# The low half of the weights begins 224 instead of 160 bytes behind the high half, modulo 256

## The chip, the cores and the metric

The kernel runs on one core of a Trainium2 chip. The metric is the device time of one execution in microseconds; it is given as the median of several executions.

## What is computed

One step of a one-layer decoder with 288 tokens (256 of a prompt, 8 sequences of 4 new ones) of width 2048. Four sub-layers stand on one residual stream, and a norm ends it:

```python
h = h + 0.5 * ((silu(hn @ wg) * (hn @ wu)) @ wd)            # FFN 1, hn = rms_norm(h), inner width 5632
h = h + concat(rms_norm(conv_y), rms_norm(attn_o)) @ w_out  # token mixing: short conv, and attention
h = h + 0.5 * ((silu(hn @ wg) * (hn @ wu)) @ wd)            # FFN 2, weights of its own
h = h + sigmoid(hn @ w_ple_gate) * (p @ w_ple_proj)         # per-layer input
y = rms_norm(h)
```

In the token mixing one projection `hn @ w_in` gives the inputs of a gated convolution of width 3 and q, k, v and the forget gates of 8 heads of 128. The prompt attends causally to itself; each sequence attends to 1024 cached rows, gathered by pages, and to its new rows. Everything is float32.

## The kernel before

Activations lie transposed: 128 features on the partitions, the 288 tokens along the row (NT = 288). All large products go through one helper, `pair` (line 311). It makes two output blocks of 128 features (b = 0, 1) from weight tiles of 4 x 128 input features by 256 output features.

**Three products for one.** So that the array's fast float32 form (fp32r) loses no accuracy, each operand is split in a high and a low part. For each input block k and output block b there are three products into the same bank of PSUM, each with 288 moving columns and a load of 128 x 128 weights:

```python
for x in (xh, xl) if rows_first else (xl, xh):
    pe.matmul(o, hi[:, j % 2, w], x, start=f, stop=False)                              # line 338
    f = False
state["product"] = pe.matmul(o, lo[:, j % 2, w], xh, start=False, stop=l)              # line 340
```

In words: low rows on high weights, high rows on high weights, high rows on low weights; then the next k. Each product has a weight load of its own, so whi is loaded twice. While a product streams its rows, the weights of the next one are loaded: whi (again) under the first product of a triple, wlo under the second, the next whi under the third. There are 5,536 such triples. `rows_first`, the other order of the first two, is used for the first pair of FFN 1 alone.

**What moves.** x (`new_x`, tile `x`, 16 blocks) is the normed input of an FFN, of w_in and of the per-layer gate; `hid` (`ffn`) holds eight inner blocks of an FFN; `zc`, `za` are the two halves of the input of w_out, in single tiles of 288; `ph`, `plo` the per-layer input. x and hid are laid out by `both` (line 212): for each block 288 high elements and behind them 288 low ones, after a pad of BEFORE_X or BEFORE_H elements.

**What is loaded.** A weight tile comes from memory in one transfer (`wraw`, 512 KB). `split_weight` (line 292) turns each half of it into `whi` (a copy on ScalarE, rounded) and `wlo` (the difference, on VectorE). Five `whi` and five `wlo` are in turn, 2,048 bytes in a partition each. Both pools are made in `build`, with a tile that nothing uses between them:

```python
wsp = pool("wsp", HALVES)
pool("low").tile([P, LOWS], F32, name="gap")
wlp = pool("wlp", HALVES)
```

**Where things lie.** Pools are placed one behind the other in a partition: constants and h, x, wraw, whi, the gap, wlo, and above them what each stage opens (f1, tq, zq, mix, cv, f2, pl). In the placed program every whi begins at a multiple of 256 bytes and every wlo at 160 modulo 256 (LOWS = 40 elements of 4 bytes). A block of whi or wlo within its tile begins 512 or 1,024 bytes on, so this holds for each load. The high rows of x begin at 240 modulo 256 (BEFORE_X = 60) and the low ones 1,152 bytes on, at 112; a block is 2,304 bytes, nine times 256, so this holds for every k. hid begins at 160 modulo 256 and its pad is 80 bytes (BEFORE_H = 20): 240 and 112 as well. Of the tiles of w_out, zc has its high rows at 160 and its low ones at 32; za has both at 160 in even blocks and both at 32 in odd ones.

The order of the work on TensorE is that of the steps in `run_steps`, with the small products of attention put between (`between`, line 1012), and two products with `meanr` for each norm (`inv_rms`, line 190).

Of the kernel before, what the change touches and what calls it, by code (L numbers as in the profile page):

```python
# [42 lines left out]

RAW = 8
HALVES = 5
LOWS = 40
BEFORE_X = 60
BEFORE_H = 20
MANUAL = False
BANKS = dict(mm=3, kt=3, va=2)  # L50
KPAIRS = (1, 8, 14, 21, 27, 34, 40, 47)
# [44 lines left out]
def build(nc, tc, ctx, A, O):  # L96
    def pool(name, bufs=1, to=ctx, **k):
        return to.enter_context(tc.tile_pool(name=name, bufs=bufs, reuse_waits="tile", **k))
# [6 lines left out]
# [3 lines that stand above are left out]
# [104 lines left out]
    def both(p, name, blocks, before, **k):  # L212
        n = blocks * 2 * NT
        t = p.tile([P, (before + n + 63) // 64 * 64], F32R, name=name, tag=name, **k)
        t = t[:, before:before + n].rearrange("p (k s n) -> p s k n", s=2, n=NT)
        return t[:, 0], t[:, 1]
# [153 lines left out]
    def do(fn):  # L370
        steps.append(([], fn))
# [18 lines left out]
    def ffn(wg, wu, wd, nextgain, work):  # L390
# [3 lines left out]
        for gi, grp in enumerate(groups):  # L394
            firstg = gi == 0 and nextgain == "norm_mix"

            def start():
                H["hi"], H["lo"] = both(work(), "hid", 8, BEFORE_H, bufs=2)
            do(start)
# [847 lines left out]
```

## Time and profile before

| | |
|---|---|
| median of 3 executions | 2280.74 us |
| the three | 2279.36, 2280.74, 2295.28 us |
| the profiled execution, its own time | 2295.44 us |
| its span, first to last instruction | 2293.7 us |
| granted TensorE clock, mean | 0.998 |
| products on TensorE | 17,387 |
| FFN 1 | about 4 to 854 us of the span |
| w_in, attention, first half of w_out | about 854 to 1290 us |
| second half of w_out | about 1290 to 1341 us |
| FFN 2 | about 1341 to 2173 us |
| per-layer input, final norm | about 2173 to 2294 us |

How to read it: a group's row gives line, engine, operation, the tile written and the tiles read, the shape and the count; then its busy time, the mean duration of one in ns, and the idle time of the engine ahead of it. For a product the tiles read are the moving rows and the weights: `mm<-x,whi` has rows of x on high weights. x and hid stand for high and low rows alike. mm, kt and va are banks of PSUM. PEld is the weight load, which runs beside PE. A row of windows gives for a stretch (us from the start of the span) its length, the busy time with the number of instructions that run in it, the granted clock, the share of the DMA engines and GB/s. The row of a single line or tile gives the shortest, the median and the longest duration in ns. Products overlap in the array, and their ends are modelled.

### The profile page before, as it was taken

What the parts mean: (1) busy time and instruction counts of PE and PEld (TensorE: products, weight loads), DVE (VectorE), ACT (ScalarE), POOL (GpSimd) and SP (SyncE); (2) the same over time, 40 slices, a digit from 0 to 9 for tenths busy, and PEclk for the clock granted to TensorE, in tenths of its full rate; (3) what the DMA queues carried; (4) which work ended last, traced back from release to release, by engine and by line L of the source; (5) the groups of instructions that cost most, each with busy time, mean ns of one, the idle gap of its engine ahead of it and who ended that gap; (6) DMA issues with size and microseconds to landing.
All of it is one profiled execution on the core that took longest, in us unless ns stands there. A gap on an engine that the chain in (4) does not pass through costs nothing.

```text
span 2293.7 us, 44307 instructions
## 1 busy us (share of the span) xinstructions
PE 2280.6 (99%) x17387; PEld 2225.6 (97%) x17387; DVE 1344.6 (59%) x2413; ACT 1051.3 (46%) x1860; POOL 323.5 (14%) x398
## 2 busy tenths in 40 slices
PE   9999999999999999999999999999999999999997
PEld 9999999999999999989888999999999999999997
DVE  7555555555555586455557775555555555555855
ACT  6444444444444463333334554444444444444654
POOL 1020000000000023345446210000000000000110
PEclk9999999999999999999999999999999999999999
DMA  8575555555555556988888554645555555555552
GB/s 273 164 246 162 170 166 166 166 166 166 165 166 166 166 164 206 346 298 297 317 317 299 183 169 150 187 155 183 172 169 167 173 166 170 171 166 172 169 170 88
DMA packets 342865, 443.37 MB, mean 193 GB/s; under 512 B 17424, under 2 KB 307104, under 8 KB 342656
## 3 DMA queue, kind: packets, MB, share of 16 engines
q1 hardware_dynamic: 320944, 366.25, 49.7%
q0 software_dynamic: 20480, 71.67, 9.0%
q8 instruction: 136, 2.23, 0.4%
q10 hardware_dynamic: 1232, 2.62, 0.3%
q14 instruction: 73, 0.60, 0.1%
HBM read 435.41 MB, written 5.07 MB: 192 GB/s over the span
## 4 chain that ended last, share of the span: by engine, by line
PE 99%; DVE 0%; ACT 0%; issue 0%; DVEq 0%
PE mm L338 62%; PE mm L340 31%; PE va L338 2%; PE va L826 1%; PE va L759 1%; PE va L340 1%; PE kt L338 0%; DVE h L1173 0%; PE kt L340 0%; PE kt L880 0%; PE kt L913 0%; PE mm L518 0%; PE kt L904 0%; PE kt L879 0%; PE mm L560 0%; PE va L839 0%
## 5 line engine op out<-in xcount | busy, mean ns | idle before, releaser
L338 PE MATMUL mm<-x,whi 128*128 128x288 f32 x7360 | 1458.7, 295 | 0.0
L292 DVE TENSOR_TENSOR wlo<-wraw,whi 128x512 fp32r<-128x512 f32 (+1 forms) x1388 | 976.2, 707 | 772.1 <-ACT whi L292 689.8
L292 ACT ACTIVATE whi<-wraw 128x512 fp32r<-128x512 f32 (+1 forms) x1388 | 866.2, 629 | 903.8 <-PE mm L338 842.6
L338 PEld LDWEIGHTS mm<-x,whi 128*128 128x128 f32 x7360 | 1171.9, 188 | 15.8 <-issue 13.5
L340 PE MATMUL mm<-x,wlo 128*128 128x288 f32 x3680 | 1077.1, 293 | 0.0
L340 PEld LDWEIGHTS mm<-x,wlo 128*128 128x128 f32 x3680 | 690.5, 188 | 0.1
L338 PE MATMUL mm<-hid,whi 128*128 128x288 f32 x2816 | 555.0, 294 | 0.0
L338 PEld LDWEIGHTS mm<-hid,whi 128*128 128x128 f32 x2816 | 448.1, 188 | 0.0
L340 PE MATMUL mm<-hid,wlo 128*128 128x288 f32 x1408 | 411.8, 292 | 0.0
L410 POOL TENSOR_TENSOR sr<-sg,rs 128x288 f32<-128x288 f32 x88 | 71.7, 816 | 1411.0 <-ACT sg L408 1410.7
L340 PEld LDWEIGHTS mm<-hid,wlo 128*128 128x128 f32 x1408 | 264.2, 188 | 0.0
L430 DVE SCALAR_TENSOR_TENSOR h<-mm,h 128x288 f32<-128x288 f32 x192 | 86.5, 455 | 21.4 <-PE mm L340 21.3
L408 ACT ACTIVATE sg<-tg 128x288 f32<-128x288 f32 x88 | 39.1, 445 | 99.4 <-DVE tg L406 99.3
L417 ACT ACTIVATE hid<-hd 128x288 fp32r<-128x288 f32 x88 | 39.2, 446 | 93.1 <-DVE hd L415 93.0
L736 POOL DMA_INDIRECT KT<-in_cache_k_dram,idx x64 | 64.2, 1003 | 116.4 <-DVE idx L166 53.6
L232 POOL TENSOR_TENSOR acc<-acc,sq 128x288 f32<-128x288 f32 x52 | 44.0, 846 | 224.4 <-ACT sq L231 222.0
L259 POOL DMA_INDIRECT page<-in_cache_v_dram,idx x64 | 64.8, 1012 | 67.6 <-PE va L826 44.4
L418 DVE TENSOR_TENSOR hid<-hd,hid 128x288 fp32r<-128x288 f32 x88 | 40.1, 457 | 22.0 <-ACT hid L417 22.0
L338 PE MATMUL va<-x,whi 128*128 128x288 f32 x256 | 52.0, 297 | 0.0
L415 DVE TENSOR_TENSOR hd<-mm,sr 128x288 f32<-128x288 f32 x86 | 39.1, 454 | 18.0 <-PE mm L340 18.0
L406 DVE TENSOR_TENSOR tg<-mm,rs 128x288 f32<-128x288 f32 x84 | 38.0, 452 | 15.4 <-PE mm L340 14.3
L207 ACT ACTIVATE x<-h,gT 128x288 fp32r<-128x288 f32 x48 | 25.5, 532 | 39.9 <-DVE h L430 24.3
(240 smaller groups left out, 1131.4 us busy)
## 6 DMA issues: line engine op xcount, KB each, us to landing
wraw<-in_w_ffn_gate_dram SPq DMA_DIRECT2D x172, 512.0 KB, 3.5
wraw<-in_w_ffn_up_dram SPq DMA_DIRECT2D x172, 512.0 KB, 3.5
wraw<-in_w_ffn_down_dram SPq DMA_DIRECT2D x160, 512.0 KB, 3.5
wraw<-in_w_in_dram SPq DMA_DIRECT2D x96, 512.0 KB, 5.1
wraw<-in_w_out_dram SPq DMA_DIRECT2D x32, 512.0 KB, 4.2
wraw<-in_w_ple_gate_dram SPq DMA_DIRECT2D x32, 512.0 KB, 3.6
wraw<-in_w_ffn_down_dram SPq DMA_DIRECT2D x32, 256.0 KB, 2.9
wraw<-in_w_ple_proj_dram SPq DMA_DIRECT2D x8, 256.0 KB, 3.1
```

Of the source, the lines that this page charges most:

```text
L232: (v if k >= KT - last_on_v else g).tensor_tensor(acc, acc, sq, ALU.add)
L259: g.indirect_dma_start(out=t, out_offset=None, in_=it["src"], in_offset=bass.IndirectOffsetOnAxis(ap=it["rows"], axis=0))
L292: for i in s.activation(hi, x, AF.Copy), v.tensor_tensor(lo, x, hi.bitcast(F32), ALU.subtract):
L338: pe.matmul(o, hi[:, j % 2, w], x, start=f, stop=False)
L340: state["product"] = pe.matmul(o, lo[:, j % 2, w], xh, start=False, stop=l)
L408: s.activation(u, t, AF.Silu)
L410: g.tensor_tensor(r, u, rs, ALU.mult)
L415: v.tensor_tensor(t, o, sg[b], ALU.mult)
L417: s.activation(H["hi"][:, k, :], t, AF.Copy)
L418: v.tensor_tensor(H["lo"][:, k, :], t, H["hi"][:, k, :].bitcast(F32), ALU.subtract)
L430: v.scalar_tensor_tensor(h[:, k, :], o, 0.5, h[:, k, :], ALU.mult, ALU.add)
L736: d = g.indirect_dma_start(out=t[:, i].rearrange("p h s -> p (h s)"), out_offset=None, in_=A["cache_k"], in_offset=bass.IndirectOffsetOnAx ...
```

## The change

Two constants are changed.

```diff
 RAW = 8
 HALVES = 5
-LOWS = 40
+LOWS = 56
 BEFORE_X = 60
-BEFORE_H = 20
+BEFORE_H = 4
 MANUAL = False
```

The gap between the pools of whi and wlo is 224 instead of 160 bytes, so every wlo begins at 224 modulo 256. All that is placed above it begins 64 bytes later. The tile of hid begins at 224 instead of 160, and its pad is 16 instead of 80 bytes, so its high rows stay at 240 and its low ones at 112. x and whi lie below the gap and stay. zc, za, ph and plo go up by 64: their rows begin at 224 and 96 instead of 160 and 32. The small tiles of VectorE, ScalarE and GpSimd in the pools of the stages (tg, sg, sr, hd, sq, tB and the like) go up by 64 too. The instructions and their order are the same on all five engines, and the sizes of tiles, buffers and transfers as well.

## The prediction

> **What bounds the kernel now.** I read the busy table first, then the costliest groups, then counts of products in long stretches, and last the order of time around one place.
>
> ```profile
> span 2293.7 us, 44307 instructions
> PE 2280.6 (99%) x17387; PEld 2225.6 (97%) x17387; DVE 1344.6 (59%) x2413; ACT 1051.3 (46%) x1860; POOL 323.5 (14%) x398
> ...
> PE 99%; DVE 0%; ACT 0%; issue 0%; DVEq 0%
> ...
> L338 PE MATMUL mm<-x,whi 128*128 128x288 f32 x7360 | 1458.7, 295 | 0.0
> ...
> L340 PE MATMUL mm<-x,wlo 128*128 128x288 f32 x3680 | 1077.1, 293 | 0.0
> ...
> L338 PE MATMUL mm<-hid,whi 128*128 128x288 f32 x2816 | 555.0, 294 | 0.0
> ...
> L340 PE MATMUL mm<-hid,wlo 128*128 128x288 f32 x1408 | 411.8, 292 | 0.0
> ```
>
> TensorE is the bound in every part: it has 99% of the span and 99% of the chain that ended last, and its large groups have 0.0 us of idle time ahead of them. Nothing is to be had from VectorE, ScalarE or the transfers; the time is the number of products times the step from the start of one to the start of the next. The mean ns of a product (291 to 298) is its whole way through the array, more than two steps long, so the step has to be taken from counts.
>
> ```profile
> 50.00:850.00 800.00, 800.00 (x6036) 1.00 0.55 171
> 1350.00:2170.00 820.00, 820.00 (x6310) 1.00 0.54 169
> 1292.00:1340.00 48.00, 48.00 (x362) 1.00 0.51 163
> ```
>
> The bracket counts the products in a stretch, with the two or so that began before it and still run (295 ns over a step of 130). First FFN: 800.00 / (6036 - 2.2) = 132.6 ns a product. Second FFN: 820.00 / (6310 - 2.2) = 130.0 ns. The attention half of the output projection: 48.00 / (362 - 2.2) = 133.4 ns. The two FFNs run the same loop, on the same shapes, at the same addresses modulo 256, under a granted clock of 1.00. So there are **two rhythms for one layout**, 2.6 ns a product apart. The order of time shows where one becomes the other:
>
> ```profile
> 1347.79 0.29 PE L340 MATMUL va<-x,wlo 128*128 128x288 f32 x1
> ...
> 1348.18 0.29 PE L340 MATMUL va<-x,wlo 128*128 128x288 f32 x1
> ...
> 1348.59 0.29 PE L340 MATMUL va<-x,wlo 128*128 128x288 f32 x1
> ...
> 1348.98 0.29 PE L340 MATMUL va<-x,wlo 128*128 128x288 f32 x1
> 1349.11 0.30 PE L190 MATMUL kt<-sqh,meanr 128*128 128x288 f32 x1
> 1349.25 0.29 PE L190 MATMUL kt<-sql,meanr 128*128 128x288 f32 x1
> ...
> 1349.65 0.30 PE L340 MATMUL va<-x,wlo 128*128 128x288 f32 x1
> ...
> 1350.04 0.29 PE L340 MATMUL va<-x,wlo 128*128 128x288 f32 x1
> ...
> 1350.44 0.29 PE L340 MATMUL va<-x,wlo 128*128 128x288 f32 x1
> ...
> 1350.82 0.29 PE L340 MATMUL va<-x,wlo 128*128 128x288 f32 x1
> ```
>
> From one low product to the next there are three steps: 0.39, 0.41, 0.39 us before the two foreign products of L190, and 0.39, 0.40, 0.38 after them. TensorE never stops there. A small shift in time was enough to change the rhythm, and it then lasts to the end of the FFN, 820 us. So the step is not set by the addresses alone, nor by VectorE or the transfers, but by how the reads of one product meet the load of the next weights, and that meeting repeats itself until something disturbs it.
>
> **The profiled execution against the median.** It took 2295.44 us for its span of 2293.7 us (1.7 us around it). The median is 2280.74 and the three times are 2279.36, 2280.74 and 2295.28. If the first FFN had the second one's rhythm, the profiled execution would be shorter by 6034 x 2.6 ns = 15.7 us: 2279.7 us, which is the lower pair of times within 1.1 us. I take it that the median has both FFNs in the fast rhythm, and that the two long ones have one FFN in the slow one. So I price the change from 2280.7, and count an FFN that changes its rhythm at 16 us.
>
> **The change part by part.** No instruction is added, removed or moved on any engine: what changes are addresses. The low weights and all that is placed above them go up by 64 bytes, and the pad ahead of the FFN's inner rows shrinks by 64 bytes. Bytes, transfers and buffers stay as they are, so DVE, ACT, POOL and the queues cost nothing more; they have cover too (DVE 59% busy, no wait of theirs on the chain).
>
> Of three steps, whose loads are those of the next product, one sees another position. While xl streams against whi, whi is loaded again: x low at 112 modulo 256, whi at 0, unchanged. While xh streams against whi, wlo is loaded: 240 against 160 before, 240 against 224 now, so the rows begin 16 instead of 80 bytes ahead of the weights. While xh streams against wlo, the next whi is loaded: 240 against 0, unchanged. The middle step comes once for each low product on x or hid:
>
> ```profile
> L340 PE MATMUL va<-x,wlo 128*128 128x288 f32 x128 | 38.0, 297 | 0.0
> ...
> L340 PE MATMUL kt<-x,wlo 128*128 128x288 f32 x32 | 9.6, 299 | 0.0
> ```
>
> With these, 3680 + 1408 + 128 + 32 = 5248 steps. In the output projection and the per-layer input both the moving rows and wlo go up by 64; there the middle step is unchanged, and the other two see whi from 64 bytes further on. Those are 288 triples, 5% of all, and I leave them at nothing.
>
> What can one such step cost? No row shows the position 16, so I bound it by the shortest and the longest product of the same kind and shape, in 80 us of either FFN:
>
> ```profile
> L338 PE MATMUL mm<-x,whi x404: 293/295/300, 399.8 to 479.9; 128*128 128x288 f32 x135
> L338 PE MATMUL mm<-x,whi x412: 289/293/296, 1879.8 to 1959.9; 128*128 128x288 f32 x138
> ```
>
> A mean product of 295 ns goes with a step of 132.6 in the first FFN, so way and step differ by about 162 ns; the shortest way of 289 is a step of 127, the longest of 300 a step of 138. From 130.5 (261 ns for the two high products of a fast triple of 390, if the low one has 129) the middle step could fall by 3.5 ns or rise by 7.5. Over 5248 steps that is -18 us or +39 us.
>
> Which value? My estimate rests on a count of meetings. In a step the product reads 288 x 4 = 1152 bytes of each partition and the load 128 x 4 = 512. If both run through the whole step, the rows gain 640 bytes on the weights and pass them modulo 256 two or three times. A start 80 ahead passes after 176 and 432 bytes of gain: twice. A start 16 ahead passes after 240 and 496: twice. 112 gives two, 240 gives three. So a triple has 7 meetings now and 7 after the change. The attention half of the output projection, whose tiles begin at 160 or 32, has 9 in its even blocks and 6 or 7 in its odd ones, nearly 8 in the mean, and its 133.4 ns is the longest step of the three stretches: more meetings, more time. With the count unchanged I take **0 us** for the middle step, inside -18 and +39. The nearest measured thing, the same loop with other meetings, lies within 2.6 ns a product.
>
> The sum: 2280.7 + 0 (middle steps) + 0 (other engines) = **2281 us**.
>
> Two rules of the Trainium skill bear on this. Its page "SBUF — State Buffer", section "Who interferes with whom", says that TensorE waits for nobody and reads moving rows and weights through two independent ports; by it an address would cost nothing at all. This trace differs: 133.4, 132.6 and 130.0 ns for one shape in three stretches. The page "TensorE: Matmul & The Clock Gate", section "Back-to-back issue gap", gives columns / 2.4 + 2.5 ns, which for 288 columns is 122.5; by it the middle steps could fall by 8 ns at most, 42 us, to an estimate of 2239. No step in the rows above is as short as that.
>
> **The rivals.**
>
> *Slower: the meeting comes too late in the step.* At 16 bytes the second meeting comes after 496 of 640 bytes of gain, where it was 432; nearer to the end of the load. If the last rows of the load are held up there, the low product, which needs those weights, begins late, and the fast rhythm can't be held: it decides as soon as the load ends after the stream of the product ahead of it. Price: both FFNs at 132.6 gives 2280.7 + 15.7 + 16.4 = 2313 us; at the longest step, 39 us, 2320. For it: the parts that are disturbed often are in the slow rhythm already, and of three stretches only one is fast. Against it: the load's own duration hardly varies in the trace.
>
> ```profile
> L340 PEld LDWEIGHTS mm<-x,wlo x3680: 186/188/192, 31.2 to 2278.0; 128*128 128x128 f32 x194
> L340 PEld LDWEIGHTS mm<-hid,wlo x1408: 186/188/189, 82.5 to 2165.0; 128*128 128x128 f32 x176
> ```
>
> *Faster: one meeting falls out.* The load may be done before the rows have gained 496 bytes; then the middle step has one meeting instead of two and ends near 127 ns: -18 us. If the stretches outside the FFNs, some 1300 triples, then took the fast rhythm too, 3900 x 2.6 = 10 us more: 2253. For it: loads of 188 ns are shorter than products of 293. Against it: 240 against 0 meets first after 16 bytes, and that step would have to show the opposite.
>
> *The change doesn't do what it says: the position of wlo plays no part*, and the two rhythms come from something else in time alone. Then 2281, with the same step counts as now, and 2297 where one FFN is slow.
>
> **How the numbers follow.** Forecast, both rhythms as long as now: 0.38, 2281 us, and 2297 if one FFN of the median execution is slow, both within 1%. wlo plays no part: 0.08, the same times. Slower by the late meeting: 0.34, 2304 to 2325. Faster: 0.20, 2245 to 2258. About 1% (22.8 us) is what a measurement of this kernel can tell from no change, since its own times differ by 0.7%. So faster 0.20, same 0.46, slower 0.34. The range of 2256 to 2318 holds the bounds of the middle step nearly whole (2263 to 2320) and two slow FFNs (2313), and leaves out the larger part of the faster case and the end of the slower one. The likeliest case alone has 2276 to 2299.
>
> **What would show it right or wrong.** Right: the stretch 1350 to 2170 us holds 6310 products within 20, or 50 to 850 us holds 6036 or 6154 of them, and no third rhythm appears. The ways of x,whi in an FFN stay between 289 and 300 ns. The late meeting is shown if both FFNs have 132 ns or more and the longest ways of x,whi go over 300; the lost meeting if the counts rise above 6340. The sum fails if one of the two unchanged steps, whi on xl or whi on xh, moves while the middle one stays: then what counts is not how many meetings a step has but what the step ahead of it leaves behind. DVE, ACT and POOL busy times must stay within 1%; if they move, the 64 bytes touch more than TensorE's reads.

## The result and the profile after

| | before | changed |
|---|---|---|
| executions | 10 | 10 |
| median | 2287.9 us | 2273.64 us |
| lowest to highest | 2279.32 to 2296.52 | 2273.14 to 2275.29 |
| profiled execution | 2295.44 us | 2274.55 us |

The ratio of the changed kernel to the one before is 0.994, with a 95% interval of 0.9914 to 0.9965: faster, by 0.35 to 0.86%. The median before isn't the same as in the three executions that the prediction had: with ten, five lie from 2279.3 to 2280.7 us and five from 2295.1 to 2296.5. The changed kernel has no such two groups. It is 6 us below the lower group (its middle value is 2279.7) and 22 us below the upper one (2295.4). In the experiments below, one execution of the kernel before (5719.16 us) and one of the layout `swapped` (3196.24 us, at a granted clock of 0.65) took far longer than all others, and nothing is read from them.

The counts of products of the changed kernel, in the two FFNs and in a piece of the input projection (us from the start of the span, length, busy time and count, clock, DMA share, GB/s):

```profile
60.00:830.00 770.00, 770.00 (x5925) 1.00 0.56 175
1350.00:2150.00 800.00, 800.00 (x6156) 1.00 0.55 169
868.00:888.00 20.00, 20.00 (x156) 1.00 0.66 214
```

The same three of the kernel before, the last at the same work, 15 us later:

```profile
60.00:830.00 770.00, 770.00 (x5809) 1.00 0.55 171
1350.00:2150.00 800.00, 800.00 (x6156) 1.00 0.54 169
883.00:903.00 20.00, 20.00 (x153) 1.00 0.65 211
```

With 2.2 taken from each count, FFN 1 goes from 132.6 to 130.0 ns a product, FFN 2 stays at 130.0, and the input projection goes from 132.6 to 130.0 (in so short a stretch one product more or less is 0.9 ns). The slow rhythm is gone from both FFNs; the fast one is no faster than it was. The costliest groups of the changed kernel tell the same in the mean ns, weakly, since an average over both FFNs hides half of it:

```profile
PE 2258.2 (99%) x17387; PEld 2203.0 (97%) x17387; DVE 1343.8 (59%) x2413; ACT 1050.4 (46%) x1860; POOL 323.5 (14%) x398
...
L338 PE MATMUL mm<-x,whi 128*128 128x288 f32 x7360 | 1443.3, 293 | 0.0
...
L340 PE MATMUL mm<-x,wlo 128*128 128x288 f32 x3680 | 1076.8, 293 | 0.0
...
L338 PE MATMUL mm<-hid,whi 128*128 128x288 f32 x2816 | 549.5, 292 | 0.0
...
L340 PE MATMUL mm<-hid,wlo 128*128 128x288 f32 x1408 | 411.8, 292 | 0.0
```

TensorE loses 22.4 us of busy time, and 1.4 us of it come back as a single wait for a whi; DVE, ACT and POOL stay within 0.1%. Where the time came from is read from the first and the last start of a few tiles (shortest, median, longest ns, then the two starts). Before:

```profile
L560 PE MATMUL mm<-h,wg x32: 406/406/430, 859.1 to 860.8; 128*32 128x288 f32 x32
L338 PE MATMUL mm<-zcl,whi x128: 291/298/484, 1223.0 to 1289.6; 128*128 128x288 f32 x128
L338 PE MATMUL mm<-zal,whi x128: 293/297/298, 1290.0 to 1340.8; 128*128 128x288 f32 x128
L338 PE MATMUL mm<-plo,whi x32: 291/296/298, 2178.0 to 2279.5; 128*128 128x288 f32 x32
```

After:

```profile
L560 PE MATMUL mm<-h,wg x32: 406/406/430, 844.2 to 845.9; 128*32 128x288 f32 x32
L338 PE MATMUL mm<-zcl,whi x128: 293/293/486, 1204.4 to 1270.6; 128*128 128x288 f32 x128
L338 PE MATMUL mm<-zal,whi x128: 295/298/299, 1271.0 to 1321.4; 128*128 128x288 f32 x128
L338 PE MATMUL mm<-plo,whi x32: 293/294/295, 2158.5 to 2258.6; 128*128 128x288 f32 x32
```

| part | before, us | after, us | difference |
|---|---|---|---|
| start to the gate logits (FFN 1 and the first projections) | 859.1 | 844.2 | -14.9 |
| to the output projection | 363.9 | 360.2 | -3.7 |
| output projection | 117.8 | 117.0 | -0.8 |
| FFN 2, to the per-layer input | 837.2 | 837.1 | -0.1 |
| per-layer input | 101.5 | 100.1 | -1.4 |

The sum is -20.9 us, and the two spans (2293.7 and 2272.7) differ by 21.0. Without FFN 1 it is -6.0, the distance to the lower group of before. So the upper group of before goes with an FFN in the slow rhythm, and the lower group lost 6 us in the other parts. This is worked out from the sum: no execution of before from the lower group was profiled. Of the other parts the input projection has just been seen to leave the slow rhythm.

### The profile page after: what moved, and what is told of

Same layout as the page of the kernel before. It is cut to its first block, busy times and chain, and to the rows that moved or that the text cites. A ratio compares the mean times of both kernels' runs of the same rounds, so it can differ in the third digit from the quotient of the medians.

```text
span 2272.7 us, 44307 instructions
## 1 busy us (share of the span) xinstructions
PE 2258.2 (99%) x17387; PEld 2203.0 (97%) x17387; DVE 1343.8 (59%) x2413; ACT 1050.4 (46%) x1860; POOL 323.5 (14%) x398
## 4 chain that ended last, share of the span: by engine, by line
PE 99%; DVE 0%; DMA 0%; ACT 0%; SPq 0%; issue 0%; DVEq 0%; ACTq 0%
PE mm L338 62%; PE mm L340 31%; PE va L338 1%; PE va L826 1%; PE va L759 1%; PE va L340 1%; PE kt L338 0%; DMA h<-in_x_dram 0%; DVE h L1173 0%; PE kt L340 0%; PE kt L880 0%; PE kt L913 0%; PE kt L904 0%; PE kt L879 0%; PE mm L560 0%; PE va L839 0%
## 5 line engine op out<-in xcount | busy, mean ns | idle before, releaser
L338 PE MATMUL mm<-x,whi 128*128 128x288 f32 x7360 | 1443.3, 293 | 0.0
L338 PE MATMUL mm<-hid,whi 128*128 128x288 f32 x2816 | 549.5, 292 | 0.0
```

## The experiments

All times are medians of 4 to 10 executions; the ratio is to the kernel before on the same chip, both groups together. There, before has its groups at 2281 to 2282 and 2297 to 2298 us, some 2 to 3 us above those of the table. In each run with other positions a second constant keeps hid at the same place as x.

### What of the change is at work

Only wlo is moved; a second gap brings all that is above back to its old place.

```diff
-LOWS = 40
+LOWS = 56
...
     wlp = pool("wlp", HALVES)
+    pool("high").tile([P, 48], F32, name="gap2")
```

> Only wlo moves to 224 modulo 256; everything above it is brought back to its old place modulo 256 by a second gap of 192 bytes. Theory of the relative position (rows of x or hid against the wlo that is loaded under them, 16 instead of 80 bytes): the slow rhythm of 132.6 ns is gone in both FFNs, about 6036 + 130 products from 50 to 850 us, 2272 to 2277 us in every execution. Theory of the weights alone (wlo against whi, 224 instead of 160): the same. Theory of the tiles above (zc, za, ph and the small tiles): as before the change, 2280 or 2296 us, with a stretch at 132.6. Theory of chance (both rhythms are still there, and the draw was lucky): some execution at 2290 or more.

Measured: 2276.95 us (2276.53 to 2277.4), ratio 0.9953 (0.9928 to 0.9977), one group, 5 us below the lower group of before. In its FFNs:

```profile
60.00:830.00 770.00, 770.00 (x5926) 1.00 0.56 175
1350.00:2150.00 800.00, 800.00 (x6156) 1.00 0.54 169
```

The counterpart leaves wlo where it was and moves what is above it, with hid's rows kept at 240:

```diff
-BEFORE_H = 20
+BEFORE_H = 4
...
     wlp = pool("wlp", HALVES)
+    pool("high").tile([P, 16], F32, name="gap2")
```

> wlo stays at 160; what lies above goes up by 64 bytes through a second gap behind wlo, and the pad of hid is 16 bytes so that its rows stay at 240. Theories of the relative position and of the weights alone: both rhythms as before, 2280 or 2296 us, up to 5 us off for zc and za. Theory of the tiles above: 2272 to 2277 us and no stretch at 132.6 ns.

Measured: 2296.15 us, in two groups (2280.9 to 2281.7, and 2295.8 to 2297.3), ratio 1.001 (0.9977 to 1.0043). The profiled execution took 2297.27:

```profile
60.00:830.00 770.00, 770.00 (x5809) 1.00 0.55 171
1350.00:2150.00 800.00, 800.00 (x6155) 1.00 0.54 170
```

The place of wlo alone does nearly all of it, 5.3 of 6.0 us. The tiles above play no part in the rhythm. Chance is no likely account either: twenty executions with wlo at 224 (ten of the change, ten of this run) show no upper group.

### Is there one slow rhythm, or two that a shift in time exchanges?

One to three stray products go in at the start of each group of an FFN but the first. That is ten places, not nine as the expectation says, five in each FFN, with 2, 3, 1, 2 and 3 of them.

```diff
+    def stray(n):
+        b = ktbank()
+        for i in range(n):
+            pe.matmul(b[:, :NT], meanr, sqh, start=i == 0, stop=i == n - 1)
...
             do(start)
+            if gi:
+                do(lambda gi=gi: stray(gi % 3 + 1))
```

> The kernel before, with one to three stray products (meanr on sqh, into a bank nobody reads) at the start of each group of both FFNs but the first: nine places (four or five in each FFN), some 2.5 us of work. Theory of a rhythm that a shift in time can change: after some of the strays the step changes between 130.0 and 132.6 ns, and both are seen within one FFN; 2283 to 2315 us. If the rhythm is fixed by something in each FFN (its pool, its weights): each FFN keeps one step through all its groups, but for a short stretch behind a stray.

Measured on before: 2296.67 us (2295.29 to 2298.82), ratio 1.0038 (1.0006 to 1.007). A stretch within each of the six groups of FFN 1:

```profile
60.00:115.00 55.00, 55.00 (x425) 1.00 0.55 169
125.00:230.00 105.00, 105.00 (x794) 1.00 0.63 206
240.00:380.00 140.00, 140.00 (x1079) 1.00 0.54 169
390.00:530.00 140.00, 140.00 (x1079) 1.00 0.54 169
540.00:680.00 140.00, 140.00 (x1058) 1.00 0.53 166
695.00:835.00 140.00, 140.00 (x1079) 1.00 0.53 168
```

In ns a product: 130.1, 132.6, 130.0, 130.0, 132.6, 130.0. Two strays turn the fast rhythm into the slow one, three turn it back, one leaves it; from then on nothing changes until the next place. One and two were met from the fast rhythm only, three from the slow one only. By the starts of the products FFN 2 does the same: triples of 390.0 ns, then 397.8, 390.0, 390.0, 397.8, 390.0. The loop and all places modulo 256 are the same all along. So the layout of before has two rhythms that hold themselves, and what goes ahead decides which one holds. That the start of an FFN is decided in the same way is argued from this, not shown.

> The changed kernel with the same strays. Theory that the new position of wlo leaves one rhythm only: 130.0 ns comes back behind every stray, 2276 to 2279 us in every execution. Theory of chance (the slow rhythm is still there and was not met): 132.6 ns or another longer step is seen behind at least one of the strays, over 2283 us.

The same strays in the changed kernel: 2280.42 us (2279.73 to 2281.36), ratio 0.9956 (0.9926 to 0.9987). The lower group of before is 2282.2 us on this chip, 2.5 above that of the table; 2273.6 + 2.5 + 22 strays of 0.13 us makes 2279.0, so 1.4 us are left for all ten disturbances. The same six stretches:

```profile
60.00:115.00 55.00, 55.00 (x425) 1.00 0.56 172
125.00:230.00 105.00, 104.29 (x800) 1.00 0.64 208
240.00:380.00 140.00, 140.00 (x1079) 1.00 0.54 170
390.00:530.00 140.00, 140.00 (x1079) 1.00 0.54 170
540.00:680.00 140.00, 140.00 (x1079) 1.00 0.54 170
695.00:835.00 140.00, 140.00 (x1079) 1.00 0.54 168
```

In five of them it is 130.0 or 130.1 ns; in the second, TensorE stood still for 0.71 us near 133 us, and (105.00 - 0.71) / (800 - 2.2) is 130.7. By the starts of the products two triples there took 0.99 and 0.96 us, and the others ahead and behind have 390.0 ns. In FFN 2 there are 6155 products from 1350 to 2150 us, one less than without strays. Behind none of the ten places is there a slow rhythm.

Then three strays once, near 56 us, in the kernel before:

```diff
+                if firstg and pi == 2:
+                    do(lambda: stray(3))
```

> The kernel before, with three stray products once, at the start of the third pair of FFN 1 (near 70 us). In the run with strays at nine places two of them turned the fast rhythm into the slow one and three turned the slow one into the fast one, in both FFNs. If that is a rule of the phase, FFN 1 is fast behind this place in every execution, whichever rhythm it began with: 2279 to 2284 us, no execution near 2296; the two times of before are then the two rhythms of FFN 1 and nothing else. If three strays from the fast rhythm lead to the slow one, or the two times have another cause: both 2281 and 2297 are still seen.

Measured: 2297.02 us in two groups, three executions from 2281.7 to 2282.1 and seven from 2295.9 to 2298.0; ratio 1.0014 (0.9983 to 1.0046). The profiled one, 2281.67, was slow ahead of the strays (8.00 / (62 - 2.2) = 133.8 ns, where one product more or less is 2 ns; by the starts its triples there have 397 to 398 ns) and fast behind them (130.0). With nearly all of FFN 1 in the fast rhythm its time lies in the lower group:

```profile
48.00:56.00 8.00, 8.00 (x62) 1.00 0.50 143
60.00:830.00 770.00, 770.00 (x5925) 1.00 0.55 175
```

The expectation that three strays always lead to the fast rhythm failed. Turning slow into fast is seen once more. What rhythm the seven long executions had on either side of the strays was not recorded. That three strays turn fast into slow as well would explain them, but is not shown.

### Which distance decides?

Six other layouts, with wlo, x or both moved, and one kernel without loads of wlo (it computes high rows on high weights a second time). "High" and "low" are the places of x's and hid's rows modulo 256, whi lies at 0. A triple is three steps; its length is worked out from the count in 1350 to 2150 us, as 3 x 800 / (count - 2.2); the 398 of before is 3 x 770 / (5809 - 2.2). Meetings are counted as in the prediction.

| run | edit | high, low | wlo | rows ahead of the load: step 1, 2, 3 | meetings | triple, ns |
|---|---|---|---|---|---|---|
| before | | 240, 112 | 160 | 112, 80, 240 | 7 | 390 and 398 |
| changed | | 240, 112 | 224 | 112, 16, 240 | 7 | 390 |
| low32 | LOWS 8 | 240, 112 | 32 | 112, 208, 240 | 8 | 391 |
| low96 | LOWS 24 | 240, 112 | 96 | 112, 144, 240 | 8 | 393 |
| low192 | LOWS 48 | 240, 112 | 192 | 112, 48, 240 | 7 | 393 |
| x48 | LOWS 56, BEFORE_X 12 | 48, 176 | 224 | 176, 80, 48 | 7 | 397 |
| x176 | LOWS 40, BEFORE_X 44 | 176, 48 | 160 | 48, 16, 176 | 7 | 400 |
| swapped | LOWS 24, BEFORE_X 28 | 112, 240 | 96 | 240, 16, 112 | 7 | 397 |
| allhi | third product on whi | 240, 112 | (not loaded) | 112, 240, 240 | 8 | 397 |

> wlo stays at 160; the high rows of x and hid go to 176, so they begin 16 bytes ahead of wlo as after the change, and 176 (high) and 48 (low) ahead of whi instead of 240 and 112. If the distance to wlo decides alone: one rhythm near 130 ns, 2270 to 2280 us. If the distance of wlo to whi decides: both rhythms as before. If the two distances to whi weigh as much: a rhythm of its own, between 130 and 134 ns, 2275 to 2325 us.

Measured: 2326.15 us (2325.97 to 2326.66), ratio 1.0159 (1.0105 to 1.0213).

```profile
60.00:830.00 770.00, 770.00 (x5777) 1.00 0.54 171
1350.00:2150.00 800.00, 800.00 (x6002) 1.00 0.53 165
```

133.3 ns a product in both FFNs, one rhythm. The distance of 16 to wlo is no good by itself.

> wlo at 224 as after the change, but the high rows of x and hid at 48, so they begin 80 bytes ahead of wlo as before the change, and 48 (high) and 176 (low) ahead of whi. If the distance to wlo decides alone: two rhythms, 130.0 and 132.6 ns, 2280 or 2296 us. If wlo against whi decides: one rhythm, 2272 to 2277 us. If the distances to whi weigh as much: a rhythm of its own, 2275 to 2325 us.

Measured: 2308.99 us (2307.92 to 2309.92), ratio 1.0086 (1.0058 to 1.0115): 6052 products in 1350 to 2150, 132.2 ns in both FFNs. wlo 224 behind whi is no good by itself either. By the Trainium skill's page "SBUF — State Buffer", section "Who interferes with whom", where TensorE waits for nobody, none of these moves would cost anything; these two cost 27 and 44 us more than the lower group of before.

> wlo at 96 modulo 256, x and hid at 240: the middle step's rows begin 144 bytes ahead. By the count of meetings (112, 368, 624: three) the middle step has one more than now: a rhythm of 133 ns or more, 2310 us or more. By the theory that the positions combine in a rhythm that no single distance tells, anything from 390 to 403 ns a triple: 2274 to 2330 us.

Measured: 2293.25 us (2292.78 to 2295.01), ratio 1.0023 (0.9993 to 1.0053), 6104 products in 1350 to 2150, 131.1 ns in both FFNs.

> wlo at 32 modulo 256, x and hid at 240: the middle step's rows begin 208 bytes ahead. By the count of meetings (48, 304, 560: three) one more than now: 133 ns or more, 2310 us or more. By the theory that no single distance tells it: 390 to 403 ns a triple, 2274 to 2330 us.

Measured: 2282.62 us (2281.86 to 2283.81), ratio 0.9943 (0.9922 to 0.9963), 130.4 ns in both:

```profile
1350.00:2150.00 800.00, 800.00 (x6138) 1.00 0.54 168
```

Both have one meeting more than the layout of before and are faster than its slow rhythm.

> wlo at 192 modulo 256, half of the way: the middle step's rows begin 48 bytes ahead. If the slow rhythm ends somewhere between 80 and 16 and nothing else happens there: either two rhythms as before (2281 and 2297) or one at 130.0 ns (2272 to 2278). If the distance in units of less than 64 bytes counts (80 and 16 are the same modulo 64, 48 is not): a rhythm of its own, 2278 to 2325 us.

Measured: 2291.27 us (2290.63 to 2291.99), ratio 1.0003 (0.9977 to 1.0029), one group, again 6104 products and 131.1 ns in both FFNs. Neither the old rhythms nor that of the changed kernel: 80, 48 and 16 don't lie on one line. The starts of the products, over some 200 triples of an FFN, tell more. In the fast rhythm of before the three steps have 130.3, 131.0 and 128.7 ns; here they have 126.7, 130.0 and 136.7. Only the distance of the middle step was moved, and the step behind it, whose own distance is still 240, got 8 ns longer.

> High rows of x and hid at 112 and low rows at 240 (changed places), wlo at 96: the three distances of a triple are the same as after the change, but the first and the third are exchanged (240, 16, 112 instead of 112, 16, 240). If each distance has a cost of its own that adds up: 390 ns a triple, about 2274 to 2278 us. If what a step leaves behind decides what the next one costs: another rhythm, up to 400 ns, 2280 to 2325 us.

Measured: 2308.68 us (2308.17 to 2309.56), ratio 1.008 (1.0048 to 1.0112), 132.2 ns in both:

```profile
60.00:830.00 770.00, 770.00 (x5826) 1.00 0.55 172
1350.00:2150.00 800.00, 800.00 (x6053) 1.00 0.53 166
```

These are the three distances of the changed kernel, with the first and the third exchanged, and a triple is 7 ns longer. A cost of each distance by itself, added up, is ruled out by this pair. That the order is what counts is not shown, since the places themselves differ too.

> The kernel before, but the third product of each triple reads the high weights again, so all loads lie at 0 modulo 256 and the middle step's distance is 240; the part of the product with the low weights is left out of the result. Theory that wlo at 160 makes the slow rhythm possible: no stretch at 132.6 ns, one rhythm in both FFNs. Theory that the slow rhythm belongs to the two steps under whi (112 and 240), which are unchanged: both rhythms are still met, 390 and 398 ns a triple.

Measured: 2307.44 us (2306.7 to 2308.11), ratio 1.008 (1.0049 to 1.0111), 6052 products in 1350 to 2150, one rhythm of 132.2 ns. With the load of wlo gone neither the 390 nor the 398 ns of before is left, so neither rhythm is a matter of the two steps under whi alone.

## Why the prediction was wrong, point by point

**Right: the bound and what could move.** TensorE has 99% of both spans, the other engines' busy times are the same to 0.1%, and all of the 21 us lies in steps of TensorE. FFN 2 holds 130.0 ns on both sides.

**Right: two rhythms for one layout, and one FFN in the slow one makes the upper group.** The prediction worked out 15.7 us from two counts. The groups of before are 15.7 us apart, and FFN 1 gave back 14.9 up to the gate logits. That a small disturbance can change the rhythm was an argument from one place with two foreign products; the strays show it.

**Wrong: the 0 us for the middle step.** This is the term that failed. It rested on the count of meetings: 7 now and 7 after, so nothing changes. Seven meetings came out at 390, 393, 397, 398 and 400 ns, eight at 391, 393 and 397. The count doesn't order them. It let rows and load run through one step alike, where the records have a load of 188 and a product of 293 ns against a step of 130, and it gave each step a cost of its own. The agreement that made it plausible (nearly 8 meetings and 133.4 ns in the output projection) was one point. In truth the change took away the slow rhythm: 14.9 us up to the gate logits in the profiled execution, whose first FFN had it, and 6 us behind. Even within the fast rhythm the middle step went from 131.0 to 129.5 ns and the third, whose distance stayed, from 128.7 to 130.5; only the triple stayed at 390.0. The prediction names a move of a step with an unchanged distance as a sign that what the step ahead leaves behind counts, and that is what is seen here and in `low192`.

**Wrong: "Forecast, both rhythms as long as now".** There is one left: the slow one is met behind none of ten disturbances and in none of ten executions. The signs that the prediction set for being right were met all the same: 6309 products from 1350 to 2170 us, ways of x,whi from 289 to 297 ns, no other length of a triple in the FFNs. They ask for either rhythm in one profile, so a kernel that has lost one of the two passes them. Nor does it speak for the mechanism that 2273.6 us lies in the range of 2256 to 2318: the range was drawn for other cases, and the likeliest one alone had 2276 to 2299.

**The rival on the fast side had the right second half and the wrong first.** It let one meeting fall out (-18 us) and then the stretches outside the FFNs take the fast rhythm (-10 us). The middle step fell by 1.5 ns instead of 3.5, and the third took it back: the fast triple stays at 390 ns. Of the second half 6 us came. It was a consequence of nothing that the rival named, and it is smaller than the 10 because not all of those stretches reach the fast rhythm: the second half of the output projection goes from 400 to 397 ns a triple (50.8 and 50.4 us for 127 of them).

**The slower rival** had its place, a late second meeting at 16. It isn't there in the changed kernel. Longer triples came from other layouts (x176, x48, swapped), where the steps under whi see other distances.

**The price from 2280.7.** Three executions, two of them in the lower group by luck, were too few to see that half of the times lie 16 us higher. Against the lower group the change gains 0.27% (6.05 of 2279.7), against the upper 0.9%; 0.994 is the mixture.

**Open.** What in the reads and the loads holds a rhythm, and why 16 has one rhythm where 80 has two, is not shown. No rule tried here (count of meetings, the one distance to wlo, wlo against whi, a sum over distances) gives the lengths of the table. Moving wlo moves the writes of VectorE as well as the loads of TensorE; the run without loads of wlo, where the writes stay, speaks for the loads, but the writes were never moved alone. All blocks differ by multiples of 256 bytes and share one length; whether a smaller unit than 256 would do was not tested as such. What sets the rhythm at the start of FFN 1, so that before falls in one group or the other, was not found.

## What to carry to other kernels

When TensorE is busy all the time, take the step from counts in long stretches of equal work, and compare stretches: two values for one shape mean that a layout has more than one rhythm, and its time will depend on the execution. A layout is worth testing with a few stray products between equal groups of work: one that returns to the same step behind each, as the changed kernel did at ten places, is less likely to be fast by luck alone. Places modulo 256 bytes of the moving rows and of both kinds of weights have to be chosen together and measured; here they were worth 2.6% of a step (390 to 400 ns a triple), and no rule for one of them alone held.

## What the runs showed of the hardware that was not expected

- The step of a product with 288 moving columns and a 128 x 128 load of float32 took 130.0 to 133.3 ns in the mean, by the places of rows and weights modulo 256, with a granted clock of 1.00. Single steps of a triple had 126.7 to 136.7 ns (`low192`), and moving the place of one load changed the step behind it by 8 ns.
- One layout can have two lengths (130.0 and 132.6 ns) that hold for some 800 us each. Two stray products turned the first into the second, three the second into the first.
- Moving wlo alone by 64 bytes ended this (2276.53 to 2277.4 us). With the tiles above it moved instead, those of VectorE, ScalarE and GpSimd among them, both groups stayed (2281 and 2297 us).
- The same three distances gave 390 ns in one order and 397 in the other.
